# Feed-forward of a two-layer trunk step on one core: groups of four blocks by seven block products instead of eight, with the gated products kept in DRAM

## The chip, the cores and the metric

One core of a Trainium2 chip runs the whole kernel. The metric is device time in microseconds of one execution; the time before is the median of three runs. PE is the matmul engine, PEld its weight load, DVE, ACT and POOL the vector, scalar and GpSimd engines, SP the engine that issues nearly all transfers.

## What is computed

One inference step of two trunk layers on 640 tokens (128 of context, 512 latent), D_MODEL 1024, D_FF 2816. A layer mixes the normalised tokens by three branches, adds the projected result to x, and then runs the feed-forward, which is what the change touches:

```python
def conv_ffn(h, w_up, conv_w, conv_b, w_down):
    u = h @ w_up                                   # 1024 -> 2 x 2816
    g, val = u[..., :D_FF], u[..., D_FF:]
    gp = jnp.pad(g, ((0, 0), (1, 1), (0, 0)))
    g = gp[:, :-2] * conv_w[0] + gp[:, 1:-1] * conv_w[1] + gp[:, 2:] * conv_w[2] + conv_b
    return (jax.nn.silu(g) * val) @ w_down         # 2816 -> 1024

# in trunk_layer
h2 = rms_norm(x, p['g_norm_ffn']) * (1 + sc2) + sh2
x = x + g2 * conv_ffn(h2, p['w_up'], p['conv_w'], p['conv_b'], p['w_down'])
```

## The kernel before

Activations lie with channels on the 128 partitions and the 640 tokens in the free dimension, in two halves of 320 (`HT`). Every float32 operand is held as two rounded parts, a high and a low one, and a product takes three matmuls (high by high, high by low, low by high). `split` (L251, L252) makes the parts: ACT copies the high part, DVE subtracts it from the value for the low part. `load` brings a weight block of 128 output channels by 8 k blocks (128x1024, 512 KB) into a `ws` buffer (three of them), `weights` splits it into `wh` and `wl` (two each).

`dense` (L270) computes one output block of 128 channels: per k block three matmuls, each on both token halves, 48 in all, into one PSUM tile `mm`. `dense_half` (L287) does the same for one half at a time, `dense_first` runs three blocks side by side at the start of a feed-forward. `modulate` (L571 to L574) makes the normalised, modulated tokens `hh` and `hl` on DVE and ACT; it is called by token halves behind the statistics of the projection before it.

The feed-forward is `ffn`. It goes over the 22 blocks f of D_FF in chunks of 9, 8 and 5 (`CHUNKS`). For each f: the gate block (48 matmuls), evicted by ACT into `gp` (L1146), convolved with three taps (L1148, L1150, L1151 on DVE), tanh (L1152, ACT), the SiLU product (L1153, L1154), then the value block (48 matmuls), multiplied in straight out of PSUM (L1159), and the result split into two `u` tiles that stay in SBUF. At a chunk's end the chunk's part of w_down is applied for the eight output blocks, each with 6 matmuls per f, and `residual` (L580) adds the result times its gate to x. The last chunk goes through `project`, half by half, so that the next norm can begin. In layer 0, the modulation vectors of later use (`ada`, L524) are computed beside this, spread in by `along` at a share of 0.15; their weights come through the same `ws` buffers.

A scheduler orders the instructions of each engine's queue from the order of the program and its own estimates; transfers are issued from SP's queue. No POOL step of the feed-forward before does more than clear three columns of `gp` (L1141).

Of the kernel before, what the change touches and what calls it, by code (L numbers as in the profile page):

```python
# [9 lines left out]
F32 = mybir.dt.float32  # L10
F32R = mybir.dt.float32r
# [9 lines left out]
KT = 8  # L21
# [12 lines left out]
CHUNKS = (9, 8, 5)  # L34
# [35 lines left out]
def _constants():  # L70
# [13 lines left out]
    # rows of a quadrant: 0.. the high part, 16.. the low part of a value  # L84
# [23 lines left out]
class WList:  # L108
    """weights of k tiles that lie in more than one block, read like (hi, lo) of one"""
# [15 lines left out]

class Feed:
    """Generators one after another; a Feed of a Feed does not end it when dropped."""
# [16 lines left out]
class Kern:  # L144
    def __init__(self, tc, ins, outs, st):
# [8 lines left out]
        self.hh, self.hl = [self.pg.tile([P, KT, T], F32R, name=t) for t in ("hh", "hl")]  # L154
        self.h = [(self.hh[:, j], self.hl[:, j]) for j in range(KT)]
# [10 lines left out]
    # -------- phases: which tiles SBUF's last part and PSUM hold  # L166
# [8 lines left out]
    def psum(self, mode):  # L175
# [7 lines left out]
        self.dense_tag = "mm" if mode == "dense" else "d"  # L183

    # -------- tiles
    def g(self, cols=T, dt=F32, name="g", x=False):
        """a [128, 640] tile, of the phase's own (x) where it has some"""
        n = NX.get(self.ph_name)
        if x and n:
            return self.ph.tile([P, T if self.ph_name == "A" else PW], dt, tag="gx", bufs=n, name=self.nm(name))[:, :cols]  # L190
        return self.pg.tile([P, T], dt, tag="g", bufs=NG, name=self.nm(name))[:, :cols]
# [13 lines left out]
    def sm(self):  # L205
        return self.pt1("sm", 2) if self.psum_mode == "dense" else self.pt1("o", 1)
# [4 lines left out]
    # -------- weights: f32 block -> (hi, lo)  # L211
# [13 lines left out]
    def weights(self, src, kt, n, h=None, out=None, ws=None):  # L225
# [3 lines left out]
        # beside attention in two steps, which keep its own steps waiting less  # L229
# [5 lines left out]
    def weights3(self, src, ws=None):  # L235
        """a further block of [128, 8, 128], split into four of the g tiles"""
# [10 lines left out]
    def split(self, src, out=None):  # L247
        """src (f32, SBUF or PSUM) -> hi, lo tiles."""
# [6 lines left out]
    # -------- dense: out[m cols, 640 tokens]; ev(psum view, h) takes the result away, h None for both halves  # L255
    def dense(self, w, acts, ev, m=P, wcol=0, tag=None):
# [4 lines left out]
        whole = tag != "d"  # L261
        for part in ((0, 1),) if whole else ((0,), (1,)):
            self.tiles += 1
            ps = self.mm() if whole else self.pt1("d", 1)
# [29 lines left out]
    def dense_first(self, jobs):  # L294
        """jobs (weights, ev) on the modulated norm, side by side: the first halves of all, then the second ones"""
        self.finish()
        ps = [self.mm() for _ in jobs]
        for h in range(2):
            gens = [
                self.dense_half(p[:, h, :HT], w, self.h, h, ev=lambda _, h, p=p, ev=ev: ev(p[:, :, :HT], None) if h else None)  # L300
# [19 lines left out]
    def pieces(h):  # L320
        """(segment, token slice, psum index) of what a psum view of half h (None: both) holds."""
# [18 lines left out]
    def rsqrt(self, ps, half=None):  # L340
        """1 / sqrt(ps + eps) of the chunks of 160 tokens, a chunk's only on its rows of rdiag, in two parts"""
# [15 lines left out]
    def newton(self, v, r, t, hs=None, sign=None):  # L357
        """r = (2 v) ** -0.5; hs the signed high part of one close to it"""
# [17 lines left out]
    # -------- setup  # L376
    def setup(self):
# [17 lines left out]
        # the first modulation's weights and the tokens, in the order of their use  # L395
# [112 lines left out]
    # -------- adaLN  # L508
# [5 lines left out]
    def ada(self, l, v):  # L514
# [31 lines left out]
    # -------- trunk norm, by token halves  # L546
# [5 lines left out]
    def norm(self, h, ps, sc, sh):  # L552
        """half h of the modulated norm, from its statistics; the second step wants the tensor engine back"""
# [29 lines left out]
    # -------- rope on the latent columns of a [n, >=640] f32 tile  # L583
# [789 lines left out]
```

## Time and profile before

| | |
|---|---|
| runs | 2317.84, 2319.34, 2321.84 us; median 2319.34 |
| profiled execution | span 2318.4 us from first to last instruction (the page gives no other time of it) |
| PE busy | 2256.9 us, 97%, 15863 instructions |
| DVE, ACT, POOL busy | 1246.9 (54%), 830.5 (36%), 150.9 us (7%) |
| feed-forward layer 0, layer 1 | 682.9 to 1203.4 us, 1825.7 to 2305.6 us of the span |
| DMA | 224.69 MB, mean 97 GB/s |

An engine is busy from an instruction's start to its end; queue handling does not count. Matmuls overlap in the records, so a pair's two starts, not one matmul's duration, give the pace. The clock line counts tenths of TensorE's full granted clock, where 9 is 90% or more.

### The profile page before, as it was taken

The page shows a single profiled execution, that of the slowest core. Times are in us where ns is not written, and L with a number is a line of the kernel's source. Part 1 is how long each engine was busy: PE and PEld are TensorE (multiplying, and loading weights), DVE is VectorE, ACT ScalarE, POOL GpSimd, SP SyncE. Part 2 cuts the span into 40 slices and gives each one's busy share as a digit, 9 for nine tenths or more (in the row PEclk, how much of TensorE's full clock was granted, in tenths as well). Part 3 has the DMA queues.
Part 4 walks back from the last instruction along what each step waited for, and adds up shares of the span by engine and source line. Part 5 has one row for each costly group of instructions (what it writes and reads, how often), then busy time and mean ns, then how long its engine had stood idle before and what let it go on. Part 6 is the DMA issues. An engine that isn't in the chain of part 4 may idle for free.

```text
span 2318.4 us, 38736 instructions
## 1 busy us (share of the span) xinstructions
PE 2256.9 (97%) x15863; PEld 2118.1 (91%) x15863; DVE 1246.9 (54%) x2262; ACT 830.5 (36%) x1578; POOL 150.9 (7%) x365
## 2 busy tenths in 40 slices
PE   7999999999999999999999999999999999999998
PEld 4898999998988888999988989999998999999997
DVE  5676736652555432543577767376535654354353
ACT  4466325541423211221334663255423332132132
POOL 1122001210000000000001220021100000000000
PEclk8999999999999999999999999999999999999999
DMA  8242343126505665322142423321124022222221
GB/s 306 69 104 53 99 117 92 46 57 194 177 12 182 189 181 172 98 78 73 55 127 69 104 52 98 82 57 52 46 80 149 23 78 82 73 73 74 74 66 62
DMA packets 283249, 224.69 MB, mean 97 GB/s; under 512 B 12223, under 2 KB 256694, under 8 KB 283072
## 3 DMA queue, kind: packets, MB, share of 16 engines
q1 hardware_dynamic: 282400, 221.43, 33.4%
q8 instruction: 125, 2.05, 0.4%
q0 software_dynamic: 672, 0.79, 0.1%
q14 instruction: 52, 0.43, 0.1%
HBM read 195.54 MB, written 8.29 MB: 88 GB/s over the span
## 4 chain that ended last, share of the span: by engine, by line
PE 81%; DVE 6%; ACT 4%; DMA 3%; issue 2%; POOL 0%; DVEq 0%; ACTq 0%
PE mm L270 50%; PE mm L287 8%; PE d L270 8%; PE o L728 3%; PE pt L637 3%; PE sm L524 2%; PE s L270 1%; DMA ws<-in_w_out 1%; ACT wh L251 1%; PE sm L335 1%; PE s L1012 1%; PE s L1013 1%; PE s L1014 1%; PE s L832 1%; DVE wl L252 1%
## 5 line engine op out<-in xcount | busy, mean ns | idle before, releaser
L252 DVE TENSOR_TENSOR wl<-ws,wh 128x1024 fp32r<-128x1024 f32 (+3 forms) x276 | 277.2, 1009 | 483.5 <-ACT wh L251 469.4
L251 ACT ACTIVATE wh<-ws 128x1024 fp32r<-128x1024 f32 (+3 forms) x276 | 242.8, 886 | 801.6 <-PE mm L270 556.0
L270 PE MATMUL mm<-hh,wh 128*128 128x320 f32 (+1 forms) x2016 | 466.6, 312 | 4.5 <-ACT wh L251 1.5
L270 PE MATMUL mm<-hh,wl 128*128 128x320 f32 (+1 forms) x2016 | 462.0, 310 | 0.8 <-DVE wl L252 0.7
L270 PE MATMUL mm<-hl,wh 128*128 128x320 f32 (+1 forms) x2016 | 461.1, 310 | 0.0
L270 PEld LDWEIGHTS mm<-hh,wh 128*128 128x128 f32 (+1 forms) x2016 | 333.8, 187 | 28.5 <-issue 21.5
L270 PEld LDWEIGHTS mm<-hh,wl 128*128 128x128 f32 (+1 forms) x2016 | 335.4, 187 | 4.6 <-DVE wl L252 1.9
L270 PEld LDWEIGHTS mm<-hl,wh 128*128 128x128 f32 (+1 forms) x2016 | 335.5, 187 | 2.2 <-issue 1.0
L270 PE MATMUL mm<-u,wh 128*128 128x320 f32 x1024 | 193.1, 310 | 0.0
L270 PEld LDWEIGHTS mm<-u,wh 128*128 128x128 f32 x1024 | 160.1, 188 | 6.2 <-issue 6.2
L626 POOL TENSOR_SCALAR p<-p,st 128x640 f32<-128x640 f32 (+1 forms) x160 | 117.8, 737 | 612.6 <-DVE st L625 556.9
L642 DVE TENSOR_TENSOR ptl<-pt,pth 128x512 fp32r<-128x512 f32 (+1 forms) x208 | 118.4, 584 | 46.2 <-PE o L728 23.2
L624 ACT ACTIVATE p<-s,st 128x640 f32<-128x640 f32 (+1 forms) x160 | 113.4, 709 | 67.0 <-DVE st L623 61.5
L641 ACT ACTIVATE pth<-pt 128x512 fp32r<-128x512 f32 (+1 forms) x208 | 103.8, 514 | 66.5 <-PE pt L637 64.7
L623 DVE TENSOR_REDUCE st<-s 128x1 f32<-128x640 f32 (+1 forms) x160 | 113.8, 711 | 21.7 <-PE s L1014 9.2
L580 DVE SCALAR_TENSOR_TENSOR x<-mm,g2h,x 128x128 f32<-128x128 f32 (+2 forms) x144 | 55.9, 434 | 128.2 <-PE mm L270 99.3
L287 PE MATMUL mm<-hh,wr 128*128 128x320 f32 x512 | 118.3, 313 | 3.2 <-ACT hh L251 3.2
L270 PE MATMUL d<-hh,wh 128*128 128x320 f32 x352 | 118.4, 336 | 2.3 <-ACT wh L251 0.5
L270 PE MATMUL mm<-u,wl 128*128 128x320 f32 x512 | 116.5, 308 | 0.0
L637 PE MATMUL pt<-ident,p 128*128 128x128 f32 x672 | 110.1, 276 | 5.7 <-DVE ptl L642 4.4
L270 PE MATMUL d<-hh,wl 128*128 128x320 f32 x352 | 109.5, 311 | 0.0
L270 PE MATMUL d<-hl,wh 128*128 128x320 f32 x352 | 109.3, 310 | 0.0
(312 smaller groups left out, 3954.2 us busy)
## 6 DMA issues: line engine op xcount, KB each, us to landing
wa<-in_w_ada SPq DMA_DIRECT2D x96, 512.0 KB, 3.9
ws<-in_w_up SPq DMA_DIRECT2D x88, 512.0 KB, 3.9
ws<-in_w_in SPq DMA_DIRECT2D x74, 512.0 KB, 4.0
ws<-in_w_down SPq DMA_DIRECT2D x34, 512.0 KB, 4.2
ws<-in_w_out SPq DMA_DIRECT2D x16, 512.0 KB, 4.2
xd<-x SPq DMA_DIRECT2D x16, 320.0 KB, 4.5
x<-xd SPq DMA_DIRECT2D x16, 320.0 KB, 6.5
ws<-in_w_down SPq DMA_DIRECT2D x16, 320.0 KB, 3.2
```

Of the source, the lines that this page charges most:

```text
L251: nc.scalar.activation(hi, src, AF.Copy)
L252: nc.vector.tensor_tensor(lo, src, hi.bitcast(F32), ALU.subtract)
L270: nc.tensor.matmul(dst, lhsT, r[:, HT * h:HT * h + HT], start=first, stop=last)
L287: nc.tensor.matmul(ps, lhsT, r[:, HT * h:HT * h + HT], start=first, stop=last)
L580: self.nc.vector.scalar_tensor_tensor(self.x[j][:, xs], ps[pi], gate[:, j, s:s + 1], self.x[j][:, xs], ALU.mult, ALU.add)
L623: nc.vector.tensor_reduce(st[:, 0:1], s, axis=AX.XY if len(s.shape) == 3 else AX.X, op=ALU.max, negate=True)
L624: nc.scalar.activation(self.half(p) if len(s.shape) == 3 else p, s, AF.Exp, bias=st[:, 0:1], accum_out=st[:, 1:2])
L626: nc.gpsimd.tensor_scalar(p, p, st[:, 2:3], 1.0, ALU.mult, ALU.mult)
L637: nc.tensor.transpose(pt[:, P * t:P * t + P], p, self.ident)
L641: nc.scalar.activation(hi, v, AF.Copy)
L642: nc.vector.tensor_tensor(lo, v, hi.bitcast(F32), ALU.subtract)
L728: nc.tensor.matmul(state["o"][:, 256 * u:256 * u + 256], vl[a](t + 1), hl[r][:, t, :], start=t == 0 and r == 0, stop=t == 4 and r == 1)
```

## The change

Of the 22 blocks f, the first two are computed as before (`PLAIN_F`). The other 20 gate blocks, the 20 value blocks, and the w_down outputs of the chunks f 0 to 7 and f 8 to 15 (`CHUNKS` is now 8, 8, 6) become 28 jobs per layer. A job is two output blocks by both token halves: four result tiles of 128x320, from eight k blocks taken as two groups of four. Eight products of 12 matmuls (96) become seven (84), by Winograd's form of Strassen's scheme: some of the seven use sums of weight blocks and sums of activation blocks, and the results are added up behind PE.

- Weight side, per job: four sums of 128x512 on POOL (`fast_sum`, L1225), done in place in the loaded blocks, and seven splits of 128x512 (`fast_split`; ACT and DVE, L276 and L277) where two of 128x1024 stood.
- Activation side, per operand set (the normed tokens, u of f 0 to 7, u of f 8 to 15): 16 differences of 128x320 on POOL (`mix_b`, L1195) and 16 to 28 splits of 128x320 into `hq` and `tq` (the second and third set have to replace the set that the running job still reads).
- Result side: per job three ACT copies out of PSUM (L1280) and three DVE additions (L1431 gate, L1454 value, L1501 down). Three of four value multiplications move to POOL (L1449), since the values now lie in SBUF.
- `fast` runs the products of all jobs in 7 slots per job, in the order 1, 2, 6, 5, 7, 4, 3, the last two among the next job's, and calls the preparation by `PREP_AT`, in slots relative to a job's first. Six PSUM banks `q` take the products.
- The products u go to DRAM (`ud`, 320 KB each) and come back as float32 (`ul`) for the down jobs; x is spilled to DRAM in the feed-forward and fetched again (`spill`, `unspill`, 8 transfers each way per layer).
- `project` for the last chunk (6 blocks) loads and splits each weight block for either token half anew, two ahead (`put=None`).
- In the modulation for the feed-forward the shift is added on POOL (L605) into `hf`, kept for `mix_b`, and split from there. The `ada` weights of layer 0's feed-forward get two buffers of their own (`wa`).

Matmuls of the program: 15177 before, 14505 now. The core of the diff (deleted comments and plain moves are left out):

```diff
-CHUNKS = (9, 8, 5)
+PLAIN_F = 2
+CHUNKS = (8, 8, 6)
...
+WSIDE = {"1": "11", "2": "12", "6": "2", "5": "1", "7": "3", "4": "22", "3": "4"}
+VSIDE = {"1": "11", "2": "21", "6": "2", "5": "1", "7": "3", "4": "4", "3": "22"}
+SLOTS = {"1": 0, "2": 1, "6": 3, "5": 4, "7": 6, "4": 9, "3": 12}
+PREP_AT = {
+    "load": (-10, -8), "22": -4, "11": -3.75, "12": -3.5, "s1": -3.75, "s3": -3.25, "s2": -3, "s4": -2.75,
+    "2": -1, "1": -0.75, "3": 0.25, "4": 0.75}
...
     def modulate(self, sc, sh, h):
...
+            if self.hf is not None:
...
+                    nc.vector.scalar_tensor_tensor(
+                        t[:, ts], self.x[j][:, ts], sc[:, j, s:s + 1], self.rb[:, ts], ALU.mult, ALU.mult)
+                    nc.gpsimd.tensor_scalar(t[:, ts], t[:, ts], sh[:, j, s:s + 1], 0.0, ALU.add, ALU.add)
+                self.split(t[:, sl], out=(hh[:, sl], hl[:, sl]))
...
     def project(self, srcs, kt, acts, gate, after, put, stat):
...
+                if put is None:
+                    n = KT * h + j
+                    while len(ws) < min(n + 2, 2 * KT):
+                        ws.append(self.weights(srcs(len(ws) % KT), kt, P))
+                    w = ws[n]
...
+    def mix_b(self, f32, n, k):
+        b = self.blocks(f32, k)
+        d, x, y = {"1": ("11", "12", "11"), "3": ("12", "22", "12"), "2": ("11", "22", "11"), "4": ("21", "21", "11")}[n]
+        self.nc.gpsimd.tensor_tensor(b[d], b[x], b[y], ALU.subtract)
...
+    def fast_sum(self, job, n):
+        a = job["a"]
+        d, x, y, op = {
+            "1": ("22", "21", "22", ALU.add), "3": ("21", "11", "21", ALU.subtract),
+            "2": ("11", "22", "11", ALU.subtract), "4": ("12", "12", "11", ALU.subtract)}[n]
+        self.nc.gpsimd.tensor_tensor(a[d], a[x], a[y], op)
...
+    def fast(self, jobs):
...
+        def done(job, n):
+            ev = job["ev"]
+            if n == "1":
+                copy(job, "m", job["x"])
+            elif n == "2":
+                ev["c11"](job["m"], job["z"], post)
+            elif n == "6":
+                copy(job, "u2", job["x"])
+            elif n == "7":
+                copy(job, "u3", job["x"])
+                ev["c22"](job["u3"], job["y"], post)
+            elif n == "4":
+                ev["c21"](job["x"], post)
+            elif n == "3":
+                ev["c12"](job["u2"], job["y"], post)
+            works.extend(job.get("after", {}).get(n, []))
...
+        for t, n, p in at:
+            job = jobs[n]
+            due((n, WSIDE[p]), (job["vn"], VSIDE[p]))
+            first, last = p in ("1", "2", "5"), p != "5"
...
+            for k in range(nk):
+                ks = slice(P * k, P * k + P)
+                for i, (x, y) in enumerate(((0, 0), (0, 1), (1, 0))):
+                    nc.tensor.matmul(
+                        ps, w[:, x, ks], v[:, y, k, :], start=first and k == 0 and i == 0,
+                        stop=k == nk - 1 and i == 2, skip_group_check=True)
+                step(t, k)
+                yield 408
+            done(job, p)
...
     def ffn(self, l, after, stat):
...
+        def out(f):
+            u = us.pop(f)
+            self.outs.append(lambda: nc.sync.dma_start(ud[f], u))
...
+        yield next(first)
+        self.spill()
+        f32 = [self.hf[0:4], self.hf[4:8]]
...
+        tasks = mix("1") + mix("3") + spl("1") + mix("2") + mix("4") + spl("2") + spl("3") + spl("4")
...
+            return [(None, lambda f=f: load(f)) for f in range(f0, f0 + 8)], {
+                "1": spl("11"), "2": spl("21"), "5": mix("1") + mix("3") + spl("1") + mix("2") + mix("4") + spl("2"),
+                "7": spl("3"), "4": spl("4"), "3": spl("22")}
...
+        yield from self.fast(jobs)
+        src = lambda j: self.wsrc("w_down", l, P * f0, nf, P * j, P)
+        yield from self.project(src, nf, acts, self.g2h[l], after, None, stat)
```

How the order on the engines moves, at three places. **PE, up blocks of layer 1.** Before, the end of one block and the start of the next:

```order
L270 MATMUL mm_21005<-hh,wh_21001 128x320 x2
L270 MATMUL mm_21005<-hl,wh_21001 128x320 x2
L270 MATMUL mm_21005<-hh,wl_21002 128x320 x2
L270 MATMUL mm_21070<-hh,wh_21066 128x320 x2
L270 MATMUL mm_21070<-hl,wh_21066 128x320 x2
L270 MATMUL mm_21070<-hh,wl_21067 128x320 x2
L270 MATMUL mm_21070<-hh,wh_21066 128x320 x2
```

Now, one job's products (`hq_66`, `hq_68`, `hq_69` are token operands as they are, `tq_19351` to `tq_19354` differences, `hq_67` holds weights):

```order
L1315 MATMUL q_19862<-hq_68,wl_19795 128x320 x12
L1315 MATMUL q_19733<-tq_19354,hq_67 128x320 x12
L1315 MATMUL q_19841<-tq_19352,wp_19821 128x320 x12
L1315 MATMUL q_19919<-tq_19351,wh_19832 128x320 x12
L1315 MATMUL q_19800<-hq_69,wp_19749 128x320 x12
L1315 MATMUL q_19841<-tq_19353,wl_19848 128x320 x12
L1315 MATMUL q_19981<-hq_66,wh_19902 128x320 x12
L1315 MATMUL q_20004<-hq_68,wl_19913 128x320 x12
L1315 MATMUL q_19841<-tq_19354,hq_67 128x320 x12
L1315 MATMUL q_19981<-tq_19352,wp_19959 128x320 x12
```

Each weight tile was used for two matmuls in a row; now each is used for one, twelve to a product, and the last two products of the job before stand among them (`q_19733` and `q_19800` among those into `q_19841`).

**POOL, feed-forward of layer 0.** Before, only the cleared columns:

```order
L1141 MEMSET gp_7295 128x1 x3
L1141 MEMSET gp_7300 128x1 x3
L1141 MEMSET gp_7623 128x1 x3
L1141 MEMSET gp_7783 128x1 x3
L1141 MEMSET gp_7938 128x1 x3
```

Now, where the down jobs' operands are made (`ul` are the fetched products, `ws` and `wb` the weights of a job, `u` and `vt` the last value job's):

```order
L1225 TENSOR_TENSOR wb_10542<-ws_10509,wb_10542 128x512
L1225 TENSOR_TENSOR wb_10542<-wb_10542 128x512
L1449 TENSOR_TENSOR u_1590_10531<-u_1590_10531,vt_10452 128x320
L1195 TENSOR_TENSOR ul_10667<-ul_10667 128x320
L1195 TENSOR_TENSOR ul_10667<-ul_10669,ul_10667 128x320
L1195 TENSOR_TENSOR ul_10674<-ul_10674 128x320
L1195 TENSOR_TENSOR ul_10674<-ul_10676,ul_10674 128x320
L1195 TENSOR_TENSOR ul_10681<-ul_10681 128x320
L1195 TENSOR_TENSOR ul_10681<-ul_10683,ul_10681 128x320
L1195 TENSOR_TENSOR ul_10688<-ul_10688 128x320
L1195 TENSOR_TENSOR ul_10688<-ul_10690,ul_10688 128x320
L1225 TENSOR_TENSOR ws_10657<-ws_10657 128x4x128
```

POOL's queue is in order: a job's weight sums, the sums over the activations and the last multiplications stand behind one another.

**DVE, change from the first to the second group of down jobs, layer 0.** Before, at the end of a w_down chunk and the start of the next gate block:

```order
L580 SCALAR_TENSOR_TENSOR x_6611<-mm_9197,g2h_178,x_6611 128x320
L252 TENSOR_TENSOR wl_9356<-ws_9353,wh_9355 128x1024
L580 SCALAR_TENSOR_TENSOR x_6612<-mm_9278,g2h_178,x_6612 128x128
L580 SCALAR_TENSOR_TENSOR x_6612<-mm_9278,g2h_178,x_6612 128x192
L580 SCALAR_TENSOR_TENSOR x_6612<-mm_9278,g2h_178,x_6612 128x320
L252 TENSOR_TENSOR wl_9434<-ws_9431,wh_9433 128x1024
L1148 TENSOR_SCALAR y_9423<-gp_9348,colsC,colsB 128x641
```

Now, the low parts of the new operands (`tq_7297` and `tq_7298` from `ul`) among those of the weights, the additions and the residuals:

```order
L277 TENSOR_TENSOR wp_11543<-wb_11343,wp_11543 128x512
L1501 TENSOR_TENSOR cp_11518<-cp_11518,q_11449 128x320
L277 TENSOR_TENSOR wl_11530<-ws_11299,wl_11530 128x512
L621 SCALAR_TENSOR_TENSOR x_10841<-cp_11518,g2h_180,x_10841 128x320
L277 TENSOR_TENSOR tq_7297<-ul_11308,tq_7297 128x320
L277 TENSOR_TENSOR tq_7297<-ul_11315,tq_7297 128x320
L277 TENSOR_TENSOR tq_7297<-ul_11322,tq_7297 128x320
L277 TENSOR_TENSOR tq_7297<-ul_11329,tq_7297 128x320
L277 TENSOR_TENSOR tq_7298<-ul_11308,tq_7298 128x320
L277 TENSOR_TENSOR tq_7298<-ul_11315,tq_7298 128x320
L1501 TENSOR_TENSOR cp_11546<-cp_11546,q_11548 128x320
L277 TENSOR_TENSOR tq_7298<-ul_11322,tq_7298 128x320
```

The splits of the new operand set stand between the weight splits (`wp`, `wl`) and the additions (L1501) that free the PSUM banks.

## Rows read from the trace of the kernel before

**Rows 1.** The page: span, busy time of the engines, and the clock's slices.

```profile
span 2318.4 us, 38736 instructions
PE 2256.9 (97%) x15863; PEld 2118.1 (91%) x15863; DVE 1246.9 (54%) x2262; ACT 830.5 (36%) x1578; POOL 150.9 (7%) x365
...
PEclk8999999999999999999999999999999999999999
```

**Rows 2.** The chain that ended last: shares of the span by engine.

```profile
PE 81%; DVE 6%; ACT 4%; DMA 3%; issue 2%; POOL 0%; DVEq 0%; ACTq 0%
```

**Rows 3.** Windows: stretch, length, busy us (count) PE PEld DVE ACT POOL; clock; DMA share, GB/s.

```profile
1825.70:2305.60 479.90, 476.99 (x3325) 470.42 (x3324) 226.37 (x347) 129.39 (x207) 6.35 (x69) 1.00 0.24 70
682.90:1203.40 520.50, 518.70 (x3691) 477.28 (x3690) 244.87 (x398) 136.60 (x225) 3.53 (x63) 1.00 0.43 128
800.00:900.00 100.00, 99.69 (x742) 86.14 (x741) 35.49 (x55) 18.29 (x24) 0.33 (x6) 1.00 0.61 182
1900.00:2000.00 100.00, 100.00 (x684) 100.00 (x683) 41.22 (x59) 24.66 (x36) 0.66 (x12) 1.00 0.27 79
```

**Rows 4.** Timeline, PE: half-order matmuls of L287, pairs of L270 (start, us, line).

```profile
1150.13 0.31 PE L287 MATMUL mm<-hh,wl 128*128 128x320 f32 x1
1150.27 0.31 PE L287 MATMUL mm<-hh,wh 128*128 128x320 f32 x1
...
1950.01 0.46 PE L270 MATMUL mm<-hl,wh 128*128 128x320 f32 x2
1950.30 0.46 PE L270 MATMUL mm<-hh,wl 128*128 128x320 f32 x2
```

**Rows 5.** Groups by form, DVE, ACT, POOL (count | busy, mean ns | idle before).

```profile
L252 DVE TENSOR_TENSOR wl<-ws,wh 128x512 fp32r<-128x512 f32 x64 | 43.3, 688 | 24.6 <-ACT wh L251 24.5
...
L251 ACT ACTIVATE wh<-ws 128x512 fp32r<-128x512 f32 x64 | 38.5, 626 | 32.6 <-PE d L270 15.0 <-PE mm L270 12.0 <-issue 2.2
...
L626 POOL TENSOR_SCALAR p<-p,st 128x640 f32<-128x640 f32 x128 | 103.8, 811 | 532.0 <-DVE st L625 506.9 <-PE pt L637 9.3 <-PE s L1014 8.7
L626 POOL TENSOR_SCALAR p<-p,st 128x128 f32<-128x128 f32 x32 | 14.1, 440 | 80.6 <-DVE st L625 50.0 <-DVE st L623 30.3
...
L1148 DVE TENSOR_SCALAR y<-gp,colsC,colsB 128x641 f32<-128x641 f32 x22 | 13.4, 613 | 29.0 <-ACT gp L1146 28.9
L1150 DVE SCALAR_TENSOR_TENSOR y<-gp,colsC,y 128x641 f32<-128x641 f32 x22 | 19.4, 888 | 0.7
...
L1154 DVE SCALAR_TENSOR_TENSOR u<-fth,y 128x512 f32<-128x512 f32 x44 | 30.1, 685 | 0.0
```

**Rows 6.** Timeline, DVE and POOL: long and ordinary steps of the same kinds.

```profile
405.14 0.67 DVE L252 TENSOR_TENSOR wl<-ws,wh 128x512 fp32r<-128x512 f32 x1
405.39 1.10 POOL L626 TENSOR_SCALAR p<-p,st 128x640 f32<-128x640 f32 x1 [5.87 <-DVE st L625]
...
421.40 0.49 DVE L1103 TENSOR_TENSOR m<-m,th 128x320 f32<-128x320 f32 x1
...
1534.42 0.80 POOL L626 TENSOR_SCALAR p<-p,st 128x640 f32<-128x640 f32 x1 [4.93 <-DVE st L625]
1534.56 0.99 DVE L1103 TENSOR_TENSOR m<-m,th 128x320 f32<-128x320 f32 x1
```

**Rows 7.** Windows around 530 us (columns as in the windows above).

```profile
529.00:531.00 2.00, 0.83 (x4) 0.59 (x4) 0.85 (x1) 1.06 (x1) 0.00 (x0) 1.00 0.76 303
533.00:536.10 3.10, 3.10 (x14) 3.10 (x13) 0.00 (x0) 0.00 (x0) 0.00 (x0) 0.51 0.83 300
```

**Rows 8.** Timeline, PE, around 530 us: waits in brackets, then a slower pace.

```profile
530.17 0.56 PE L270 MATMUL mm<-hh,wh 128*128 128x320 f32 x2 [1.18 <-ACT wh L251]
...
531.43 0.56 PE L270 MATMUL mm<-hh,wl 128*128 128x320 f32 x2 [0.40 <-DVE wl L252]
...
533.60 0.74 PE L270 MATMUL mm<-hh,wl 128*128 128x320 f32 x2
534.14 0.74 PE L270 MATMUL mm<-hh,wh 128*128 128x320 f32 x2
```

More of the change, by code (lines that the diff above doesn't have):

```diff
@@ new lines, in split_b, with fast_load @@
+    def split_b(self, v, f32, n, k):
+        src = self.blocks(f32, k)[{"1": "11", "2": "11", "3": "12", "4": "21"}.get(n, n)]
+        self.split(src, out=(v[n][:, 0, k, :], v[n][:, 1, k, :]))
+    def fast_load(self, job, a):
+        pool, tag, bufs = (self.pw, "ws", NWS) if a else (self.ph, "wb", 2)
+        w = pool.tile([P, 1024], F32, tag=tag, bufs=bufs, name=self.nm(tag))
+        self.nc.sync.dma_start(w.rearrange("p (k n) -> p k n", n=P), job["src"]()[a])
+        order = "p (k t n) -> p t k n" if job.get("mixed") else "p (t k n) -> p t k n"
+        if a == 0:
+            self.flush()
+        for t in range(2):
+            job["a"][f"{a + 1}{t + 1}"] = w.rearrange(order, t=2, n=P)[:, t]
@@ new lines, in flush, with fast_split @@
+    def flush(self):
+        for o in self.outs:
+            o()
+        self.outs.clear()
+    def fast_sum(self, job, n):
[4 more added lines that the diff above has]
+        self.nc.gpsimd.tensor_tensor(a[d], a[x], a[y], op)
+    def fast_split(self, job, n):
+        w = job["w"]
+        src = job["a"][{"1": "22", "2": "11", "3": "21", "4": "12"}.get(n, n)]
+        if n == "22":
+            self.n22 = 1 - self.n22
+            w[n] = self.w22[self.n22]
+        else:
+            pool, tag, bufs = WPLACE[n]
+            w[n] = (self.pw if pool else self.ph).tile([P, 1024], F32R, tag=tag, bufs=bufs, name=self.nm(tag))
+            w[n] = w[n].rearrange("p (v n) -> p v n", v=2)
+        self.split(src, out=[w[n][:, x].rearrange("p (k n) -> p k n", n=P) for x in range(2)])
@@ new lines, in value_plain, with ev @@
+        def value_plain(f):
+            def ev(ps, h):
+                for hh in range(2) if h is None else (h,):
+                    a = self.half(us[f], hh)
+                    nc.vector.tensor_tensor(a, a, ps[hh] if h is None else ps, ALU.mult)
+                if h != 0:
+                    out(f)
+            return ev
+        wpt = lambda: self.ph.tile([P, 1024], F32R, tag="wp", bufs=NWP, name=self.nm("wp"))
+        w0 = self.weights(wup(DFF), KT, P, out=(wpt(), wpt()))
+        ws = [self.weights(wup(0), KT, P), self.weights(wup(P), KT, P)]
@@ new lines, in behind @@
+        def behind(job, n, works):
+            after = job.setdefault("after", {})
+            after[n] = after.get(n, []) + works
+        for f0 in (0, 8):
+            loads, works = chunk(f0)
+            behind(jobs[-2], "6", loads)
+            if f0 == 0:
+                behind(jobs[-1], "5", [("x", self.unspill)])
+            for n, w in works.items():
+                behind(jobs[-1], n, w)
+            for j in range(0, KT, 2):
+                jobs.append({
+                    "src": lambda f0=f0, j=j: down_src(f0, j), "v": v, "vn": f0, "mixed": True,
+                    "ev": Later(lambda j=j: down_job(j))})
@@ new lines, in ffn, with last_load, last_split @@
+        f0, nf = sum(CHUNKS[:2]), CHUNKS[2]
+        acts, ul = [], {}
+        def last_load(i):
+            self.flush()
+            ul[i] = self.g(name="ul")
+            nc.sync.dma_start(ul[i], ud[f0 + i])
+        def last_split(i, slot):
+            hi, lo = [Halves([slot[:, i % 2, 2 * w + h, :] for h in range(2)]) for w in range(2)]
+            for h in range(2):
+                hs = slice(HT * h, HT * h + HT)
+                self.split(ul[i][:, hs], out=(hi[:, hs], lo[:, hs]))
+            acts.append((hi, lo))
```

330 lines of the change are left out of this document (247 added, 83 removed).

## The prediction, made before the changed kernel was run

> **What bounds the kernel now.** I read the page first: PE is busy 2256.9 of 2318.4 us, DVE 54%, ACT 36%, POOL 7%, with TensorE's granted clock full in all slices but the first [rows 1]. The chain that ended last says the same: 81% of it is PE, 6% DVE, 4% ACT [rows 2]. The windows narrow it to the stage that changes: in the feed-forward of layer 1 PE is busy 476.99 of 479.90 us, in that of layer 0 518.70 of 520.50, and 100 us in the middle hold 684 matmuls without a gap [rows 3], 0.146 us each; a pair starts every 0.29 us [rows 4]. So here only fewer matmuls save time, and DVE, ACT and POOL cost nothing as long as they stay ahead of PE. A surplus there counts, though: DVE is busy 226 us and ACT 129 us of those 480, POOL 6 [rows 3].
>
> **What the change removes.** 56 jobs (28 per layer) with 84 matmuls in place of 96: 672 x 0.1466 us = **98.5 us**. This holds only if the new order keeps the pace. Each weight tile now serves one matmul and not two, but the half-order matmuls of L287, each with a weight tile of its own, start 0.14 to 0.15 us apart [rows 4]. A product (12 matmuls) then takes 1.76 us, a job of seven 12.3 us, a gate and value pair 24.6 us, and layer 1's feed-forward would fall to 479.9 - 49.3 = 430.6 us.
>
> **What it adds: DVE and POOL steps that exclude each other.** Before, POOL does next to nothing there. Now it gets two-input steps: 112 sums of 128x512 and 78 of 128x320 per layer (48 differences, 30 multiplications). No row shows such a step. The lower bound is POOL's one-input step: 811 ns for 640 columns and 440 ns for 128 [rows 5] make a line of 0.35 us + 0.72 ns per column, so 0.72 us for 512 and 0.58 for 320. The upper price doubles the slope, one pass for each input: 1.09 and 0.81 us. I take the upper one, because DVE too is slower when two tensors are read (888 ns against 613 for the same columns [rows 5]), and keep the lower one for the range. The Trainium skill speaks against this placing of sums ("GPSIMD Engine Reference", sections 3.1 and 4.1: two-input elementwise work belongs on VectorE, GPSIMD being about twice as slow; 4497 ns for 2048 float32 columns); a quarter of that, an estimate, is 1.12 us, and the sum by it would end within 2 us of mine. No run here shows it.
>
> Now the collision. A POOL step that began while DVE made a low part from two SBUF tensors took 1.10 us instead of 0.81; DVE's subtraction had begun at 405.14 and lasted 0.67, so POOL got its turn 0.55 us after DVE's start [rows 6]. The other way, DVE's 128x320 addition took 0.99 us beside a POOL step that had begun at 1534.42, against 0.49 undisturbed, so it waited until about 0.64 us of POOL's 0.80 were over [rows 6]. So the two take turns: a 128x512 split step holds the other off for 0.55 us, a 641-column tap 0.75 (888 ns less the same 0.13), a 320 step 0.35, a POOL step its duration less 0.16: 0.93 and 0.65 us, at the low price 0.56 and 0.42. Steps of DVE that read PSUM I count as free of this.
>
> Turns of a steady gate and value pair (two jobs): DVE 14 splits x 0.55 + 4 taps x 0.75 + 2 SiLU products x 0.70 (685 ns for 512 columns [rows 5], and a small one) = 12.1 us, up to 13.0 if the first taps, which read one tensor, count; POOL 8 x 0.93 + 3 x 0.65 = 9.4 us. Together 21.5 to 22.4 of 24.6 us, some 90%; at the low price 17.8 to 18.7, some 74%. It fits, but at 90% with queues in fixed order some steps come late. I put that at 0.7 us per pair, about one POOL turn, x 20 pairs = **14 us** (low price 0).
>
> **Where it does not fit: the refills.** At the step from value jobs to down jobs, and again from the first to the second group, the new operands must be made within 19 slots (33.4 us), because the running job still reads the old ones: 28 splits x 0.35 = 9.8 us, 16 differences x 0.65 = 10.4, and the running preparation, 14 weight splits (7.7) and 8 sums (7.4) that come due by then. That is 35.3 us. At the first refill the last pair's convolutions (4.4) and multiplications (2.0) make it 41.7, or 8.3 over; at the second the residuals (8 x 0.35) make it 38.1, 4.7 over. Two layers: **26 us** (low price: 34.4 and 31.5, so 2).
>
> **The ends of a feed-forward.** At its start the modulated tokens now go DVE, POOL, ACT, DVE where it was DVE, ACT, DVE, the 16 differences and 16 splits must be made beside four plain blocks only, and the first job's weights follow a chain of splits and sums. I take one POOL and DVE round for each of the eight k blocks of one half, 8 x 0.75 = 6 us per layer, **12** (low 4). At the end the first w_down blocks of `project` are split behind the last additions, 2.5 us per layer, **5**, and each half now loads anew, which is hidden: 18 matmuls (2.6 us) per block cover a 128x768 split.
>
> **The clock.** At 530 us PE waited 1.18 and 0.40 us for weights [rows 8], being busy 0.83 us of two [rows 7]; behind that the granted clock was 0.51 for 3.1 us [rows 7], the lower of TensorE's levels, and pairs started 0.54 us apart instead of 0.29 [rows 4, 8]. That is some 1.5 us more for such a stall. At four refills: **6 us**.
>
> Work at no cost: ACT's copies (a job has ten, each at most the 0.63 us of 128x512 [rows 5]; 28 x 10 x 0.63 = 176 us on top of 129 [rows 3], of 431); the spills and `ud`, about 22 MB more per layer. Layer 0, the busier one, moves 182 GB/s at a share of 0.61 in its middle [rows 3], and 22 MB over 475 us add 47 GB/s, a share of about 0.77. If that cover fails, see below.
>
> **Sum.** 26 + 14 + 12 + 5 + 6 = 63 us lost of 98.5: a net -35.5. The profiled execution spans 2318.4 us and the runs' median is 2319.3, 0.9 above; on the median it makes **2284 us**. With the losses of this case between half and one and a half times, its own range is 2252 to 2315.
>
> **Rivals.**
> *POOL is cheap.* At the low price the losses are 2 + 0 + 4 + 5 + 4 = 15: 2319.3 - 98.5 + 15 = 2236 us. For it: POOL's one-input steps, the only ones seen. Against it: two inputs.
> *Taking turns becomes the bound (slower).* Mechanism: DVE's weight splits wait behind POOL's sums, PE waits for DVE in every pair, and the clock drops behind each wait. It decides where the pair's turns reach 24.6 us: 12.1 + 8h + 3 x 0.7h = 24.6 gives h = 1.24 us, a sum of 1.40 us. At h = 1.35 a pair takes 25.8, 1.2 late, with 1.5 of clock: 20 x 2.7 = 54 us. The refills become 50.8 and 46.3, 30 over per layer, 61 in both. Ends 20: 135 in all, so 2319.3 - 98.5 + 135 = 2356 us; at the deciding point itself about 2334. For it: 90% already, queues in order, and prices for POOL that are extrapolated. Against it: 1.40 us is twice the lower bound, and layer 0's 40 us of ada matmuls give some room. The same comes out if a step holds the other off for its whole duration: 14 x 0.69 + 4 x 0.89 + 2 x 0.98 (0.3 for the small product) + 8 x 1.09 + 3 x 0.81 = 26.4 us. This is the rule of the Trainium skill ("SBUF — State Buffer", on the shared port pair: an exclusive lock, held for the whole instruction). The trace shows 0.13 and 0.16 us less than the whole in the two collisions [rows 6], so I keep it in this rival.
> *Transfers come late in layer 0.* Two `wa` buffers, SP's queue in order with waits for products to be written, and a share of 0.77: ten late loads of 2 us with 1.5 of clock each add 35 us to the 63, which ends at no change, 2319. Against it: the share stays under 1, and loads are issued eight to ten slots ahead.
> *The change does not do what it says,* its matmuls run slower one by one: rows 4 speak against it, and I give it nothing of its own.
>
> **How the numbers follow.** The forecast 0.45, cheap POOL 0.28, turns as the bound 0.20, transfers 0.07. Predicted is the likeliest, 2284. The range takes in the cheap case with 4 us to spare (2232) and reaches into the slow one halfway between its deciding point and its price (2345). Plus or minus 0.2% (4.6 us) is what a measurement of this kernel can tell from no change. Faster: the forecast and cheap POOL, 0.73, and 0.01 of the transfers, 0.74; same: the rest of the transfers, 0.06; slower: the turns, 0.20.
>
> **What would show it.** PE 672 matmuls fewer, L1315 about 0.147 us apart, and layer 1's feed-forward near 460 us (430.6 and half of the losses) instead of 479.9. Right steps: the POOL sums (L1225) at 1.0 to 1.2 us on the mean, with DVE's 128x512 splits (L277) stretched well over 688 ns beside them; PE waiting for DVE and ACT splits at the refills, with dips of the clock there, and short waits elsewhere. POOL sums near 0.75 us and a feed-forward near 438 us would mean the cheap case; PE waits in every pair and a clock well under full through the whole stage, the slow one; waits of weight splits on DMA, the transfers. I am most wrong if DVE and POOL don't take turns for these forms, or if PE waits for something else: PSUM banks freed late behind DVE's queue.

## The result and the profile after

The change makes the kernel slower: median 2425.3 us (2425.0 to 2427.1, four runs) against 2318.6 for the kernel before in the same comparison; the ratio is 1.047, 95% interval 1.045 to 1.049. The forecast was 2284, with a range to 2345, so it failed in sign and in size. 672 matmuls are gone, as the counts on the page show (15863 before [rows 1]), and PE still ends 107 us later. So 98.5 + 106.7 = 205 us were lost, where the prediction had 63. The page of the profiled execution: its span, the busy times, and TensorE's clock in 40 slices.

```profile
span 2425.3 us, 39524 instructions
...
PE 2223.3 (92%) x15191; PEld 2065.3 (85%) x15191; DVE 1610.5 (66%) x2844; ACT 1014.8 (42%) x2078; POOL 706.2 (29%) x793
...
PEclk8999999999998999988999999999999899998899
```

PE's share falls from 97% to 92% and the clock now dips in each feed-forward; POOL's busy time rises from 151 to 706 us, DVE's from 1247 to 1611 [rows 1]. The stages of layer 1's feed-forward stand in four windows (columns as in [rows 3]): its start up to the second job, jobs 1 to 17 (all on the normed tokens), jobs 18 to 21 around the first refill of the operands, jobs 22 to 25 around the second.

```profile
1868.00:1941.10 73.10, 52.59 (x280) 48.58 (x279) 51.71 (x84) 25.68 (x55) 43.82 (x49) 0.81 0.16 49
1941.10:2181.50 240.40, 221.62 (x1430) 218.46 (x1429) 184.70 (x269) 98.30 (x205) 127.86 (x140) 0.96 0.33 97
2181.50:2258.60 77.10, 56.26 (x338) 53.52 (x337) 69.38 (x95) 32.99 (x72) 48.76 (x44) 0.89 0.43 140
2258.60:2329.00 70.40, 55.29 (x337) 53.84 (x337) 53.90 (x92) 31.12 (x69) 43.64 (x32) 0.88 0.30 96
```

Without a wait, 17 jobs of 84 matmuls take 17 x 12.31 = 209.3 us, and four jobs 49.2. The middle row lost 31 us, the two refills 28 and 21. The start holds 192 plain matmuls and one job, 28.1 + 12.3 = 40.4 us of work, and took 73.1. Layer 0 lost 14, 28 and 21 us in the same stages (its jobs 1 to 17 took 257.4 us and 243.6 in runs without waits, the rest being ada matmuls). What is left of the 205, some 62 us by subtraction, lies in the two starts and, about 5 us each, behind the jobs. What PE waited for in the whole kernel: total, times, longest.

```profile
PE q L1315 <- ACT cp L1280: 79.7, 28, 7.7
PE q L1315 <- ACT gp L1382: 18.0, 2, 9.4
...
PE q L1315 <- DVE wh L277: 11.3, 5, 2.9
```

In jobs 1 to 17 alone, first of layer 1, then of layer 0:

```profile
PE q L1315 <- ACT cp L1280: 18.6, 10, 2.6
...
PE sm L554 <- DMA wa<-in_w_ada: 7.6, 5, 2.3
PE q L1315 <- ACT cp L1280: 2.3, 1, 2.3
```

The leading wait is not for operands. PE waits for an ACT copy (`cp`, L1280) that must take a partial result out of its PSUM bank before the next product adds to it. One of these waits, in a steady pair of up jobs, from the timeline:

```profile
2017.90 0.68 DVE L277 TENSOR_TENSOR hq<-ws,hq 128x512 fp32r<-128x512 f32 x1
...
2018.66 1.29 POOL L1225 TENSOR_TENSOR ws<-ws 128x512 f32<-128x512 f32 x1 [1.24 <-DVE hq L277]
...
2020.03 1.29 POOL L1225 TENSOR_TENSOR ws<-wb,ws 128x512 f32<-128x512 f32 x1
...
2021.40 1.31 POOL L1225 TENSOR_TENSOR wb<-ws,wb 128x512 f32<-128x512 f32 x1
...
2022.74 0.63 ACT L276 ACTIVATE wp<-wb 128x512 fp32r<-128x512 f32 x1 [5.83 <-POOL wb L1225]
...
2024.62 0.42 ACT L1280 ACTIVATE cp<-q 128x320 f32<-128x320 f32 x1
...
2025.09 1.15 PE L1315 MATMUL q<-tq,hq 128*128 128x320 f32 x6 [2.07 <-ACT cp L1280]
```

DVE ends a split, and only then can POOL begin the job's first sum, since it is made in place in the block that was split. Three sums in a row end at 2022.7. ACT has been idle for 5.83 us before the split of the third, and the copy of the last job's product 7, whose matmuls ended at about 2019.5, is behind that split in ACT's queue. It runs at 2024.62, and product 4, which adds to the same bank, begins at 2025.09, 2.07 us late. Jobs 1 to 17 of layer 1 have eight such waits of 2.05 to 2.58 us, one in each pair, and two short ones; the rest of the 31 us goes with a slower clock (PE is busy 221.6 us there in place of 209.3), shown below.

The prices, by groups: POOL's first weight sum of a job, POOL's shift and one of its differences, and then DVE's steps in jobs 1 to 17 and a little beyond.

```profile
L1225 POOL TENSOR_TENSOR ws<-ws 128x512 f32<-128x512 f32 x56 | 92.0, 1643 | 199.0 <-DVE hq L277 174.0 <-DMA ud<-u 13.4 <-DMA wa<-in_w_ada 9.9
...
L605 POOL TENSOR_SCALAR hf<-hf,mod 128x320 f32<-128x320 f32 x16 | 25.1, 1576 | 14.0 <-DVE hf L603 14.0
L1195 POOL TENSOR_TENSOR hf<-hf,hf 128x320 f32<-128x320 f32 x24 | 24.2, 1032 | 1.2 <-DVE tq L277 0.9
```

```profile
L277 DVE TENSOR_TENSOR wp<-wb,wp 128x512 fp32r<-128x512 f32 x38 | 35.2, 929 | 55.4 <-ACT wp L276 55.2
L1338 DVE SCALAR_TENSOR_TENSOR y<-gp,colsD,y 128x641 f32<-128x641 f32 x18 | 29.7, 1650 | 0.3
L1337 DVE SCALAR_TENSOR_TENSOR y<-gp,colsD,y 128x641 f32<-128x641 f32 x18 | 24.2, 1343 | 0.6
```

Weight sums that begin while DVE makes no step between SBUF tensors take 1.26 to 1.31 us, as in the steady pair above, where only a step reading PSUM stands beside the first. On DVE the second and third taps, 888 ns before [rows 5], take 1.3 to 1.65 us on the mean, and the splits into `wp` 929 ns for 688.

Behind a wait of 2.08 us that ended at 1996.61, the granted clock was 0.68 on the mean of 5.4 us, so for a part of them at the lower of its two levels, and full again in the next window. Six of the eight waits have such a dip behind them; the one shown above, which ended at 2025.09, has none.

```profile
1996.60:2002.00 5.40, 5.39 (x26) 5.39 (x27) 5.37 (x11) 2.90 (x8) 1.97 (x2) 0.68 0.48 137
2002.00:2009.00 7.00, 7.00 (x50) 7.00 (x49) 5.10 (x5) 2.81 (x6) 5.72 (x4) 1.00 0.31 91
```

### The profile page after: what moved, and what is told of

Same layout as the page of the kernel before. It is cut to its first block, busy times and chain, and to the rows that moved or that the text cites. A ratio compares the mean times of both kernels' runs of the same rounds, so it can differ in the third digit from the quotient of the medians.

```text
span 2425.3 us, 39524 instructions
## 1 busy us (share of the span) xinstructions
PE 2223.3 (92%) x15191; PEld 2065.3 (85%) x15191; DVE 1610.5 (66%) x2844; ACT 1014.8 (42%) x2078; POOL 706.2 (29%) x793
## 5 line engine op out<-in xcount | busy, mean ns | idle before, releaser
L276 ACT ACTIVATE wh<-ws 128x512 fp32r<-128x512 f32 (+4 forms) x250 | 183.6, 742 | 433.8 <-PE mm L295 211.6
L277 DVE TENSOR_TENSOR wl<-ws,wh 128x1024 fp32r<-128x1024 f32 (+4 forms) x194 | 168.1, 872 | 220.9 <-ACT wh L276 205.9
L295 PE MATMUL mm<-hq,wh 128*128 128x320 f32 (+1 forms) x1472 | 281.0, 311 | 3.1 <-ACT wh L276 1.2
L295 PEld LDWEIGHTS mm<-hq,wh 128*128 128x128 f32 (+1 forms) x1472 | 227.0, 184 | 15.4 <-issue 9.3
L277 DVE TENSOR_TENSOR wp<-wb,wp 128x512 fp32r<-128x512 f32 x112 | 106.8, 955 | 154.8 <-ACT wp L276 154.4
L1315 PE MATMUL q<-tq,hq 128*128 128x320 f32 x672 | 130.0, 348 | 73.4 <-ACT cp L1280 73.2
L1315 PEld LDWEIGHTS q<-tq,hq 128*128 128x128 f32 x672 | 115.7, 216 | 83.9 <-ACT cp L1280 81.0
L276 ACT ACTIVATE wp<-wb 128x512 fp32r<-128x512 f32 x112 | 70.4, 629 | 248.5 <-POOL wb L1225 242.3
L295 PE MATMUL d<-hq,wh 128*128 128x320 f32 x704 | 168.9, 323 | 2.2 <-ACT wh L276 0.5
L295 PE MATMUL mm<-hq,wl 128*128 128x320 f32 (+1 forms) x736 | 169.5, 310 | 0.5 <-DVE wl L277 0.4
L605 POOL TENSOR_SCALAR hf<-hf,mod 128x128 f32<-128x128 f32 (+2 forms) x48 | 52.1, 1096 | 355.5 <-DVE hf L603 331.7
L1225 POOL TENSOR_TENSOR ws<-ws 128x512 f32<-128x512 f32 x56 | 92.0, 1643 | 199.0 <-DVE hq L277 174.0
L1315 PE MATMUL q<-hq,wh 128*128 128x320 f32 x672 | 114.7, 316 | 25.3 <-ACT gp L1382 18.0
L1315 PE MATMUL q<-tq,wp 128*128 128x320 f32 x672 | 122.6, 335 | 7.6 <-ACT cp L1280 5.8
L1315 PEld LDWEIGHTS q<-hq,wh 128*128 128x128 f32 x672 | 103.0, 192 | 31.1 <-ACT gp L1382 18.5
L295 PEld LDWEIGHTS mm<-hq,wl 128*128 128x128 f32 (+1 forms) x736 | 121.0, 184 | 4.0 <-issue 1.5
L312 PE MATMUL mm<-hq,wr 128*128 128x320 f32 x768 | 121.9, 312 | 2.5 <-ACT hq L276 2.5
```

The source lines that it names most:

```text
L276: nc.scalar.activation(hi, src, AF.Copy)
L277: nc.vector.tensor_tensor(lo, src, hi.bitcast(F32), ALU.subtract)
L295: nc.tensor.matmul(dst, lhsT, r[:, HT * h:HT * h + HT], start=first, stop=last)
L312: nc.tensor.matmul(ps, lhsT, r[:, HT * h:HT * h + HT], start=first, stop=last)
L605: nc.gpsimd.tensor_scalar(t[:, ts], t[:, ts], sh[:, j, s:s + 1], 0.0, ALU.add, ALU.add)
L1225: self.nc.gpsimd.tensor_tensor(a[d], a[x], a[y], op)
```

## The experiments

All are timed against the kernel before on the same chip, whose median lay between 2316.0 and 2318.3 us; a difference of 2 us between runs is therefore not read. Two theories stood at the start. A: the chain of POOL's sums, and what queues behind it on ACT, makes PE wait. B: DVE and POOL take turns, and the turns themselves fill the time, whoever waits for the sums.

**Splits behind the copies.** An added dependency for the scheduler queues each split of a summed block behind the last product copy on ACT, and their steps are called later:

```diff
+        if n in ("1", "2", "3", "4") and self.cp is not None:
+            with self.tc.issue_after(self.cp):
+                self.split(src, out=out)
...
-    "2": -1, "1": -0.75, "3": 0.25, "4": 0.75}
+    "1": 1, "2": 1.25, "3": 4, "4": 7}
```

> The ACT splits of the four weight sums are queued behind the copies of the products that run before they are needed (their steps are also called later); POOL, DVE and every count of work stay as in the changed kernel. Theory A (queue order: in ACT's queue the copy that frees a PSUM bank stands behind splits that wait for POOL's sums, so PE waits 2.1 us in each pair of up jobs and the clock falls behind it): jobs 1 to 19 of layer 1, now 12.3 to 17 us each, fall to about 12.5, some 35 us per layer, and a part of the refill waits goes too: 2330 to 2355 us. Rival B (DVE and POOL exclude each other and their turns fill the pair): the turns are as many as before, so no more than 10 us: 2415 to 2425.

Measured 2467.0 us, 42 more than the change, so neither number held. PE's waits for the copies fell from 79.7 to 14.7 us in total, but it waited 66 for the low parts `wl`, 30 for `wp` and 14 for `wh` from DVE (line numbers are one to seven higher in this kernel):

```profile
PE q L1322 <- DVE wl L278: 66.0, 44, 3.6
PE q L1322 <- DVE wp L278: 29.8, 18, 2.4
...
PE q L1322 <- ACT cp L1286: 14.7, 5, 4.2
PE q L1322 <- DVE wh L278: 13.6, 9, 3.2
```

In the timeline three sums of POOL and three steps of DVE alternate strictly:

```profile
2025.68 1.66 POOL L1226 TENSOR_TENSOR ws<-ws 128x512 f32<-128x512 f32 x1 [8.11 <-DVE hq L278]
2026.12 1.90 DVE L1344 SCALAR_TENSOR_TENSOR y<-gp,colsD,y 128x641 f32<-128x641 f32 x1
...
2027.41 1.73 POOL L1226 TENSOR_TENSOR ws<-wb,ws 128x512 f32<-128x512 f32 x1
2027.94 1.75 DVE L278 TENSOR_TENSOR wl<-ws,wl 128x512 fp32r<-128x512 f32 x1
2029.22 1.62 POOL L1226 TENSOR_TENSOR wb<-ws,wb 128x512 f32<-128x512 f32 x1
2029.61 1.91 DVE L1345 SCALAR_TENSOR_TENSOR y<-gp,colsD,y 128x641 f32<-128x641 f32 x1
2029.74 3.04 PE L1322 MATMUL q<-tq,wl 128*128 128x320 f32 x10 [2.92 <-DVE wl L278]
```

DVE's tap takes 1.90 us and its split 1.75 where they alone take 0.89 and 0.69; POOL's sums take 1.6 to 1.7 where they alone take 1.29. One POOL and one DVE step together take 1.7 to 1.8 us, about what the turns of the prediction give with the measured price (1.13 for POOL, 0.75 or 0.55 for DVE). The run does not tell A from B, though. Its splits are also called some two to six slots later, which alone can make PE wait for the low parts: on a kernel whose sums are not on POOL the same edit cost 32 us (the last tries below). What it shows is the alternation.

**The sums on DVE.** One line of `fast_sum`, `nc.gpsimd` to `nc.vector`.

> The 224 weight sums run on DVE instead of POOL. Theory A: three sums in a row take about 2.1 us on DVE instead of 3.9 on POOL, so the copies behind the splits come some 1.8 us earlier and the 2.1 us wait of each pair nearly goes, but DVE gets 77 us more per layer and becomes late at the refills: 2350 to 2390. Rival B: the pair's turns fall from about 24.4 to 20 us, all waits of the up jobs go: about 2350. Were POOL's sums not in the way at all, no change or slower by the load on DVE: 2425 or more.

Measured 2328.3, 97 us less than the change, more than either theory said. Jobs 1 to 17 of layer 1:

```profile
1893.80:2103.00 209.20, 209.20 (x1430) 209.20 (x1429) 201.99 (x343) 106.13 (x206) 38.38 (x73) 1.00 0.37 111
```

PE is busy through all 209.2 us at the full clock, and DVE, with some 76 us of sums more per layer, is 97% busy without making PE wait. The same work is cheaper on the fuller engine: a sum takes 0.68 us there in place of 1.29, and its result needs no third queue between DVE and ACT. How much of the 97 us each of these gives, this run does not show.

**The differences on DVE** (one line of `mix_b`) and **the shift on ACT** (one line of `modulate`, an activation with a bias):

> The 96 differences of activation blocks run on DVE (about 0.49 us) instead of POOL (0.94 to 1.14). Theory A: at the two refills and at the start the splits of these differences wait less, which takes 4 to 8 us off each of six places: 2380 to 2400. Rival B': at these places DVE is the full engine (88% busy there), so its load cancels what POOL's latency gave: 2415 to 2435. The steady pairs, without such steps, stay as they are by either.

> The shift of the modulated tokens is added on ACT (about 0.45 us for 320 columns) instead of POOL (1.3 to 1.6 us measured). If the start of each feed-forward, 26 us longer than before in layer 1, hangs on that POOL step: 8 to 10 us per layer less, 2405 to 2410. If it hangs on the differences and the first job's chain of sums: under 5 us in all, 2420 to 2425.

Measured 2398.4 and 2402.3: 27 and 23 us less, the first as A expected, the second more than either number. The differences cost at the refills (jobs 18 to 21 from 77.1 to 73.2 us, 22 to 25 from 70.4 to 65.6) and the starts; jobs 1 to 17 stay at 240.5. The shift gives some 12 us per layer, at the start (73.1 to 60.0 in layer 1).

**Sums that nobody waits for, and none.** To part A from B, POOL makes the same steps but into a spare strip (`self.scr`), or not at all; either way the splits read the blocks as loaded, and the sums are left out of the result. The edit of the first:

```diff
-        self.nc.gpsimd.tensor_tensor(a[d], a[x], a[y], op)
+        self.nc.gpsimd.tensor_tensor(self.scr, a[x], a[y], op)
```

> POOL makes the same 224 two-input steps of 128x512 on the same weight blocks at the same places, but writes the results to a spare strip, and the splits read the blocks as loaded (the weight sums are left out of the result). Nobody but a buffer's reload waits for a POOL sum. Theory A (the chain: three sums of 1.3 us in a row on POOL between a DVE split and an ACT split, each stretched by the turns): without anyone waiting the up jobs fall to about 12.4 us as in the run with the sums on DVE, and the whole to 2310 to 2335. Rival B (the turns alone: POOL's steps hold DVE up, whoever waits for the sums): DVE's steps beside POOL stay at 1.7 to 1.9 us, the up jobs stay at 13.5 us or more: 2370 to 2410.

> The weight sums are left out altogether, on every engine (the splits read the blocks as loaded). This is the floor for any placing of the sums. With the sums on DVE the up jobs of layer 1 already ran without a wait, so by either theory only the first jobs and the refills can gain against that run: 2300 to 2325. If it stays at 2328 or above, the sums on DVE cost nothing and all that is left are the start, the refills and the tail.

Measured 2387.2 and 2312.4. The sums on POOL cost 113 us (2425.3 less 2312.4), and 75 of them are lost even where nobody needs the result; with the wait for the results it is 38 more. So turns can cost this much with nobody waiting, as B says. But the two numbers do not divide the loss of the change itself. Jobs 1 to 17 of layer 1 in the run with unwaited sums, and PE's waits for the copies in the whole of it:

```profile
1916.50:2145.90 229.40, 215.09 (x1430) 213.26 (x1429) 225.45 (x272) 100.02 (x205) 149.09 (x144) 0.98 0.35 102
...
PE q L1315 <- ACT cp L1280: 57.6, 19, 8.1
```

20 us of the 31 remain, and DVE is busy for 225 of 229 us, much of it held off. In the change it is busy for 185 of 240: there the chain makes PE late while DVE has room, here, where the sums no longer wait for a split, DVE is full. In both PE waits most for the copies, which stand in ACT's queue behind a step that waits, for POOL's sum there and more often for DVE's tap here. So turns and queues work together, and how the 113 us divide between A and B in the change stays open.

On DVE the sums cost 16 us in all (2328.3 less 2312.4), all of it at the refills. Without sums the refills of layer 1 still take 61.7 and 57.7 us instead of 49.2 each, with DVE busy for 57 and 52 us of them; this part needs no sum:

```profile
2092.80:2154.50 61.70, 52.73 (x338) 51.68 (x337) 57.00 (x94) 34.23 (x73) 23.82 (x26) 0.92 0.51 169
2154.50:2212.20 57.70, 51.58 (x338) 50.79 (x337) 51.60 (x93) 31.16 (x68) 17.73 (x16) 0.97 0.38 117
```

**All three moves together, and POOL empty.**

> Sums and differences on DVE and the shift on ACT; POOL keeps only the value multiplications. If the three single effects (97, 27 and 23 us) were independent, 2280; since DVE is by then the fuller engine at the refills and the start, I expect two thirds of the two smaller ones: 2295 to 2310, which would be faster than the kernel before. If DVE is what bounds refills and start, 2320 to 2340.

> As the run before in this list, with the value multiplications on DVE too, so that POOL only clears columns. Each of the 60 multiplications costs DVE 0.49 us instead of holding it off for up to 1.1 us on POOL: by theory B a little faster than the run before (5 us), by load on DVE alone a little slower (5 us). It tells whether any POOL step is worth keeping.

Measured **2280.3**, ratio to the kernel before 0.984 (0.982 to 0.985): 37 us faster than that and 145 faster than the change. The three effects add up (97 + 27 + 23 = 147). With the multiplications on DVE too it is 2282.1, no difference; they may stay on POOL. Layer 1's stages, in the order of the four windows above:

```profile
1800.90:1852.60 51.70, 45.39 (x279) 42.86 (x278) 48.87 (x106) 27.93 (x66) 0.45 (x7) 0.93 0.23 69
1852.70:2062.00 209.30, 209.30 (x1430) 209.30 (x1429) 201.98 (x342) 106.15 (x206) 37.72 (x73) 1.00 0.37 111
2062.00:2124.20 62.20, 52.39 (x338) 51.11 (x338) 61.73 (x123) 34.57 (x73) 9.31 (x12) 0.95 0.53 174
2124.20:2182.30 58.10, 53.88 (x338) 51.73 (x337) 56.63 (x123) 29.17 (x66) 0.00 (x0) 0.94 0.37 116
```

The start falls by 21 us, the middle to the bare matmuls, the refills to 62.2 and 58.1. They still lose 13 and 9 us, with DVE 97 to 99% busy.

**POOL steps in the kernel before.** `weights` also gets two POOL additions of its block's halves into a strip that nobody reads. The 120 of the expectation are the blocks; the run made 236 steps.

> The kernel before, with two two-input POOL additions of 128x512 for each weight block of 128x1024 that its feed-forwards split (120 in all), written to a spare strip that nobody reads. By the turns as measured now (a POOL step of 1.29 us holds DVE off for about 1.13, a 128x1024 split holds POOL off for about 1.09) a gate and value pair has 2 x 1.09 + 4 x 1.13 and the taps, the product and the split, about 10.5 of 14.1 us: it fits with room, and PE waits for nothing new: within 5 us of the kernel before. If a POOL step beside DVE costs time whatever the room, as the 75 us for 224 unwaited steps might be read, some 40 us more.

Measured 2344.6, 26 us more: neither number. The windows tell where (the middle of layer 1's feed-forward, and 160 us of layer 0's with the ada work):

```profile
2000.00:2100.00 100.00, 100.00 (x684) 100.00 (x684) 52.62 (x60) 22.34 (x33) 38.86 (x39) 1.00 0.24 69
740.00:900.00 160.00, 150.26 (x1091) 126.30 (x1091) 67.38 (x84) 32.99 (x50) 57.62 (x52) 1.00 0.53 167
```

The second of these windows in the kernel before:

```profile
740.00:900.00 160.00, 159.69 (x1188) 138.28 (x1187) 62.82 (x92) 34.81 (x51) 1.05 (x18) 1.00 0.61 181
```

In the middle there are 684 matmuls in 100 us, as before [rows 3], with POOL 39% and DVE 53% busy: there the steps are free. The loss is at the starts and in layer 0's first part (1091 matmuls in these 160 us, 1188 in the same window before), where the ada weights share the `ws` buffers. In that window SP, before it can load ada weights, waits 92.5 us for DVE's splits and 14.6 for POOL's steps to free a buffer, where it waited 35.7 and nothing before; that these late loads make the whole loss was not tried apart.

**Two further tries on the fastest kernel.** The splits behind the copies again, and the first differences of a refill called three slots earlier:

> The fastest kernel so far (sums and differences on DVE, shift on ACT) with the splits of the summed weights queued behind the product copies on ACT, as in the first run. There the order only moved the wait, because DVE was held off by POOL. If the copies behind splits are what is left of the refills (20 us of PE waits for them), 5 to 12 us less: 2268 to 2275. If the refills hang on the splits and differences themselves, whatever their order, no change or some us more, 2278 to 2290.

> The fastest kernel so far (sums and differences on DVE, shift on ACT), with the first two differences of a refill called behind product 2 of the running job instead of behind product 5, three slots earlier. In that kernel the refills still lose 13 and 9 us per layer, with PE waiting up to 7.4 us for a copy that stands behind splits of differences in ACT's queue. If that burst of steps behind product 5 is the cause, 3 to 5 us less per refill: 2262 to 2274. If DVE is simply full there, no change: 2277 to 2284.

Measured 2312.3, 32 us more, and 2279.5, no change. The same edit thus costs 32 us without any sum on POOL, and 42 with them in the first run. Calling the first differences earlier brings nothing, as expected if DVE is full there; what would shorten the refills stays open.

## Why the prediction was wrong

- *What is removed:* right. The pace of L1315 is the old one: 1430 matmuls in 209.3 us wherever nothing waits, 0.146 us each. The rival of slower single matmuls is out.
- *The price of a POOL step:* too low, and the bounds did not hold the truth. The doubled slope gave 1.09 us for 512 columns; undisturbed sums take 1.26 to 1.31 and the shortest differences 0.86, where I had taken 0.81. The one-input row was a multiplication and no measure for other operations: the shift, one-input too, took at least 0.72 us for 128 columns and 1.35 for 320, where the line gave 0.44 and 0.58. The quarter of the Trainium skill's figure ("GPSIMD Engine Reference", section 3.1), an estimate of 1.12 us, was low as well. Scaled to 320 columns too it would give 0.70 us and a sum some 6 us smaller, not within 2 as I wrote. The Trainium skill's choice of engine (section 4.1) was right: the sums are worth 97 us on DVE.
- *The turns:* right as a mechanism. They are what the alternation in the first experiment shows; the whole-duration rule of the Trainium skill ("SBUF — State Buffer", on the shared port pair) is not borne out there: a POOL step of 1.29 us and a DVE step of 0.89 or 0.69 take 1.7 to 1.8 us together, not 2.0 to 2.2. With the measured price (1.13 and 0.71 us held) a pair's turns are 12.1 + 8 x 1.13 + 3 x 0.71 = 23.3 of 24.6 us, just under the point at which the slow rival was to decide. The pair took 28.3 (two of 17 jobs in 240.4 us).
- *"I put that at 0.7 us per pair":* this is the step that failed first. I treated the turns as a sum of time, and a sum of 90% as fitting. But a job's sums come in one burst, inside a chain (DVE split, three or four sums, ACT split, DVE low part) with the copies behind it in ACT's queue. Steady losses were 31 + 14 = 45 us, not 14 (and 6 of clock for everything): 3.7 per pair in layer 1, wait and slow clock together. Layer 0's ada matmuls did give the room that was named: its jobs 1 to 17 have one wait for a copy, of 2.3 us. Larger in us are the misses at the refills (72) and at the starts (40), below.
- *The refills,* 26 us: the place was right, the size was 98 (28 + 21 per layer). Some 20 of the 49 us per layer are there without any sum, and 22 in the fastest kernel, where POOL is nearly idle: I had set turns against 33.4 us, not DVE's whole work with its PSUM steps, and in the fastest kernel DVE is 97 to 99% busy there.
- *The start,* 12 us: some 52 in both layers. I priced POOL's shift within a round of 0.75 us; for 320 columns it took 1.35 to 2.0 us, eight times between the statistics and the second half's operands, with differences queued among them. The shift on ACT alone gave back 23.
- *The ends,* 5 us: about 10. *Transfers:* nearly right. PE waited 11.5 us for ada weights in all, 7.6 of them in layer 0's jobs 1 to 17, where the kernel with the three moves has no such wait.
- *Work at no cost:* ACT's sum of time did fit (1015 us of 2425), but its order in the queue was the place where PE lost most. I had argued from its load alone.
- *The rivals:* nearest is the slow one, at 0.20, with a wait in every pair of layer 1 and mostly the clock behind it. Its mechanism came only in part: the turns stayed under the pair's time, and PE waited not for DVE's splits but for copies on ACT. The last of my signs of being most wrong, PSUM banks freed late, is what came, behind ACT's queue and not DVE's. Its 2356 us was 69 short, for want of refills and starts at their real size. The cheap case is out.

## What to carry to other kernels

When work is moved to an idle engine, ask what it shares with the busy one and who stands behind it in the queues: here 224 sums on an engine that was 7% busy cost 113 us, and 16 on the busier DVE. A sum of turns below the stage's time does not show that they fit when the steps come in bursts inside a chain; cost the chain from the last thing it waits for to the bank or buffer it frees. A price from one operation's row of an engine is no price for another operation, so a change that rests on such a price deserves one run of that step by itself.

## What the runs showed of the hardware

POOL's time per column depends strongly on the operation: a multiplication by a column took 0.80 us for 640 columns [rows 6], an addition of a column 1.35 for 320, a two-input addition or subtraction 0.86 for 320 and 1.26 for 512 (the shortest of each, but for the first).

Not every POOL step holds DVE off. A two-input sum does, until shortly before its end: the split in the first two lines below takes 0.69 us alone, so it had its turn 0.14 us before the sum ended. But beside the shift, in the last two, a split took 0.49 us, as long as alone:

```profile
2022.78 1.27 POOL L1225 TENSOR_TENSOR wb<-wb 128x512 f32<-128x512 f32 x1
...
2023.40 1.20 DVE L277 TENSOR_TENSOR wp<-wb,wp 128x512 fp32r<-128x512 f32 x1 [4.42 <-ACT wp L276]
...
1885.15 1.36 POOL L605 TENSOR_SCALAR hf<-hf,mod 128x320 f32<-128x320 f32 x1
...
1885.71 0.49 DVE L277 TENSOR_TENSOR hq<-hf,hq 128x320 fp32r<-128x320 f32 x1 [1.76 <-ACT hq L276]
```

And DVE ran 97% busy through 209 us beside PE at full clock and pace without making it wait, so a high busy share alone was no sign of a bound.
